# A fifth landing slot for weight pieces, and the on-chip space that it takes from constants, work tiles and step sizes

## The chip, the cores and the metric

The kernel runs on one core of a Trainium2 chip (trn2). A core has five engines that run side by side and wait for each other by semaphores: TensorE (PE; its weight loads are listed as PEld), VectorE (DVE), ScalarE (ACT), GpSimd (POOL) and SyncE (SP), which here mostly issues transfers. The metric is the device time of one execution in microseconds, the median of several runs.

## The reference, cut to what matters

Two layers over 256 rows of 1024 columns. A layer has a mixer, in which a retention branch and a state-space branch (SSD) run on the same normed input, and a gated feed-forward part.

```
for l in range(DEPTH):                                   # DEPTH = 2, x is (256, 1024), float32
    u = rmsnorm(h, norm_mix_w[l]) @ w_in[l]              # q, k, v, g_ret, z, xbc, dt, gate_ret, gate_ssd
    yr = retention(rotary(q), rotary(k) * DK**-0.5, v)   # 2 chunks of 128 rows, 4 heads
    o_ret = (silu(g_ret) * head_rmsnorm(yr)) @ ret_out[l]
    xs, bm, cm = split(silu(causal_dwconv(xbc)))
    dtp = softplus(dt + dt_bias);  a = -exp(a_log)       # "step sizes", 32 heads
    ys = ssd_scan(xs * dtp, dtp * a, bm, cm) + d_skip * xs
    o_ssd = (group_rmsnorm(ys * silu(z)) * ssd_norm_w[l]) @ ssd_out[l]
    h = h + (sigmoid(gate_ret) * o_ret + sigmoid(gate_ssd) * o_ssd) @ w_o[l]
    gate, up = split(rmsnorm(h, norm_ffn_w[l]) @ w_gate_up[l])
    h = h + (silu(gate) * up) @ w_down[l]
out = rmsnorm(h, final_norm_w)
```

## The kernel before, in words

All weights pass through the chip once. A weight piece is 128 partitions by up to 1024 columns (512 KB). Its way is: SyncE's queue issues its transfer into a landing tile (raw, line 488 in feeder); ScalarE copies it, rounded, into wh (line 508, split_h); VectorE subtracts, wl = raw - wh (line 533, split_l); TensorE multiplies three times with high and low halves (mm3, lines 550 to 552; the fm jobs in lines 1036 and 1039), which gives nearly float32 accuracy at the fast rate. A landing tile is free again when wl is written. Before, there are 4 landing tiles (RB) and 7 pairs of wh and wl (HB).

The work is a list of jobs, one per block of output columns: v, gr (the gates' and dt's columns), bc and xs (the convolved columns), q, k, g, z, then ret, ssd and wo (the three output products), and the FFN's. Each has matmul steps on TensorE and a "post" that drains its sums on ScalarE and VectorE. Three job kinds matter here:

- The ssd job (out_wino) and then the wo job (out_job). Post ssd_post multiplies and adds into D on VectorE (D<-acc,D and D<-D), TensorE transposes the block (tr<-cst,D, line 646 in transposed), ScalarE copies the high half (A<-tr) and VectorE subtracts for the low half (A<-tr,A). The wo job reads both halves.
- The z jobs. z_post takes a work tile (sil), writes silu into it, multiplies by the SSD result, normalises, and lets TensorE transpose it (tr<-cst,sil). At the same time the SSD chunks run: ips (line 1769) reads xdt, yps (line 1782) reads seg and xdt.
- A norm (class Norm). square takes a work tile for the sum of squares, half takes one for the normed block (sil<-O,rstd,wb), which is transposed into xT; "plain" is a further copy of the transposed block. Only when both ScalarE copies are made is the work tile free. This happens for four blocks (2 row halves t, 2 column halves n) at each norm, and in the opening, where x arrives in four blocks while the first v pair already runs on a transposed copy of x.

The order of the instructions on each engine is not written by hand. Class Flow plays the kernel at build time with a cost for every operation: a generator asks for an operation, an event, or a semaphore (a free tile), and whenever an engine is free the ready operation with the lowest priority number is emitted. What comes out is one fixed list per engine, and on the chip each engine goes through its list in order. So a change of the number of tiles changes the lists all along the kernel. The semaphores that the change touches are rawS (landing tiles), silS (work tiles "sil", 128x512) and the small tiles of steps().

steps() computes the step sizes: softplus of dt, la = -dt * exp(a_log), and its running sums by a product with the mask le (row index at most column index) and gt (its complement). ssd_scores multiplies three blocks of scores by le, ones, le.

Of the kernel before, what the change touches and what calls it, by code (L numbers as in the profile page):

```python
# [9 lines left out]
F32 = mybir.dt.float32  # L10
F32R = mybir.dt.float32r
AF = mybir.ActivationFunctionType
ALU = mybir.AluOpType
# [3 lines left out]
P = 128  # L17
D = 1024
SEQ = 256
NT = 2  # L20
# [4 lines left out]
NH = SG * HPG  # L25
M2 = NT * NH
# [14 lines left out]
    return [at, at + 2] if c < NPAIR else [at]  # L41


K_ID, K_GT, K_LE, K_COS, K_SIN, K_DEC = 0, 128, 256, 640, 896, 1152
K_N = K_DEC + RH * SEQ


# [145 lines left out]
def trunk_kernel(  # L193
# [3 lines left out]
    ssd_out, w_o, norm_ffn_w, w_gate_up, w_gf, w_rw, w_sw, w_dw, w_down, final_norm_w, consts, out,  # L197
):
    nc = tc.nc
    HB, RB, TAIL, WARM = 7, 4, 5, 2  # L200
    LATE = 2500.0
    SLOW, MT_SLACK = 1500.0, 800.0
    ADDS = 600.0
# [7 lines left out]
    tp = ctx.enter_context(tc.tile_pool(name="tp", bufs=2))  # L211
    sp = ctx.enter_context(tc.tile_pool(name="sp", bufs=2))
# [7 lines left out]
    def act(n, pr, out, in_, func, psum=False, **kw):  # L220
        ptr = sum(hasattr(kw.get(a), "shape") for a in ("scale", "bias"))
        cost = 0.833 * n + (50 if psum else 92) + 93 * ptr + (95 if "accum_out" in kw else 0)
        return Op("act", cost, lambda: nc.scalar.activation(out=out, in_=in_, func=func, **kw),  # L223
                  pr, TABLES.get(func))
# [4 lines left out]
    def tt(n, pr, out, in0, in1, op):  # L229
        return dve(n, pr, lambda: nc.vector.tensor_tensor(out=out, in0=in0, in1=in1, op=op))  # L230
# [21 lines left out]
    def pooled(pool_, shape, dt, tag, bufs):  # L252
        sem = Sem(bufs)
        return sem, lambda name=tag: pool_.tile(list(shape), dt, tag=tag, name=name, bufs=bufs)
# [3 lines left out]
    rawS, new_raw = pooled(wp, (P, D), F32, "raw", RB)  # L258
    hlS = Sem(HB)
    ccS, new_cc = pooled(tp, (P, D), F32, "cc", 2)  # L260
    silS, new_sil = pooled(tp, (P, 512), F32, "sil", 3)
    sxS, new_sx = pooled(tp, (P, 512), F32, "sx", 4)
    sxG = Sem(1)
    segS, new_seg = pooled(tp, (P, HPG, P), F32, "seg", 2)
# [10 lines left out]
    h = [None] * NT  # L275
    cst = cp.tile([P, K_COS], F32, tag="cst", name="cst")
    ident = cst[:, K_ID : K_ID + P]
    gt = cst[:, K_GT : K_GT + P]
    le = cst[:, K_LE : K_LE + P]
    ones = cst[:, K_LE + P : K_LE + 2 * P]  # L280
    mhalf = cp.tile([P, 2], F32, tag="mhalf", name="mhalf")
    junk = cp.tile([P, 2], F32, tag="junk", name="junk")

# [1026 lines left out]
    early_par = Event()  # L1310
    first_tables = []

    def layer(l, mix, nxt, opening=None):
# [38 lines left out]
        run["v01"] = lambda: first_pair(opening, [v_post(0), v_post(1)])  # L1352


        dps = sp.tile([P, M2], F32, tag="dps", name="dps", bufs=1)
        dt_ev = [Event() for _ in range(NT)]
        sgr, sgr_ev = [None] * NT, [[Event() for _ in range(3)] for _ in range(NT)]

# [24 lines left out]
        def small(tag):  # L1383
            return sp.tile([P, M2], F32, tag=tag, name=tag, bufs=1)
# [4 lines left out]
        def steps():  # L1389
            pr = at_job[0] + 2  # L1390
            _, prm = yield par
            ea = sp.tile([P, NH], F32, tag="ea", name="ea", bufs=1)
            yield dt_ev[0]
            yield dt_ev[1]
            ax, sr, pol, dtt = small("ax"), small("sr"), small("pol"), small("dtt")
            n = M2
            yield stt(n, pr, ax, dps, -1.0, dps, ALU.mult, ALU.max)
            yield act(n, pr, ax, ax, AF.Exp, scale=-1.0)
            yield act(NH, pr, ea, prm[:, 1, :], AF.Exp)

            yield ts(n, pr, sr, ax, 2.0, None, ALU.add)
            yield dve(6 * n, pr, lambda: nc.vector.reciprocal(out=sr, in_=sr))
            yield tt(n, pr, sr, ax, sr, ALU.mult)
            yield tt(n, pr, ax, sr, sr, ALU.mult)
            cf = [2.0 / (2 * i + 1) for i in range(9)]
            yield ts(n, pr, pol, ax, cf[8], cf[7], ALU.mult, ALU.add)
            for i in range(6, -1, -1):
                yield tt(n, pr, pol, pol, ax, ALU.mult)
                yield ts(n, pr, pol, pol, cf[i], None, ALU.add)
            yield tt(n, pr, pol, pol, sr, ALU.mult)  # L1410
            yield stt(n, pr, dtt, dps, 0.0, pol, ALU.max, ALU.add)
            la = small("pol")
            yield stt(n, pr, v3(la), v3(dtt), -1.0, ea.unsqueeze(1).broadcast_to([P, NT, NH]), ALU.mult, ALU.mult)
            yield 4000.0

            yield accS

            def sums():
                ps = new_acc()
                nc.tensor.matmul(ps[:, :M2], lhsT=le, rhs=la, start=True, stop=True)  # L1420
                nc.tensor.matmul(ps[:, M2 : M2 + NH], lhsT=gt, rhs=la[:, :NH], start=True, stop=True)
                return ps

            ps = yield pe(300, pr, sums)
            acs, dec = small("ax"), small("sr")
            yield dve(n, pr, lambda: nc.vector.tensor_copy(out=acs, in_=ps[:, :M2]))
            yield act(n, pr, dec, ps[:, NH : M2 + NH], AF.Exp, psum=True)
            fl.release(accS)
            yield accS

            def sums_t():
                ps = new_acc()
                for t in range(NT):
                    nc.tensor.matmul(ps[:NH, t * P : (t + 1) * P], lhsT=la[:, t * NH : (t + 1) * NH], rhs=le,
                                     start=True, stop=True)
                return ps

            ps = yield pe(490, pr, sums_t)
            yield silS
            acsT = new_sil("acsT")[:NH, : NT * P].rearrange("p (t i) -> p t i", t=NT)  # L1440
            yield act(SEQ, pr, acsT, ps[:NH, :SEQ].rearrange("p (t i) -> p t i", t=NT), AF.Copy, psum=True)
            fl.release(accS)

            def out_dma():
                dr = drp.tile([NT, NH, P], F32, tag="acs", name="acs")
                nc.sync.dma_start(out=dr.rearrange("t h i -> h t i"), in_=acsT)
                return dr

            dr = yield Op("sp", 100, out_dma, pr)
            yield 2500.0  # L1450
            fl.release(silS)
            fl.set(steps_ev, (dtt, acs, dec, dr))
# [237 lines left out]
        def ssd_scores(g):  # L1690
            pr = at_job[0]
            for w in range(2):
                yield bc_ev[w][g // 2]
            bT, cT = bc[0].value, bc[1].value
            yield LATE
            yield cbmS
            yield accS

            def scores():
                ps = new_acc("cps")  # L1700
                nc.tensor.matmul(ps[:, :SEQ], lhsT=bT[:, g, :P], rhs=cT[:, g, :], start=True, stop=True)
                nc.tensor.matmul(ps[:, SEQ : SEQ + P], lhsT=bT[:, g, P:], rhs=cT[:, g, P:], start=True, stop=True)
                return ps

            ps = yield pe(660, pr, scores)
            cb = sp.tile([P, 3, P], F32, tag="cbm", name="cbm", bufs=SG)
            yield tt(3 * P, pr, cb, ps[:, : 3 * P].rearrange("p (b i) -> p b i", b=3),
                     cst[:, K_LE : K_LE + 3 * P].rearrange("p (b i) -> p b i", b=3), ALU.mult)
            fl.release(accS)
            cb_left[0] -= 1  # L1710
            if not cb_left[0]:
                fl.release(bigS["D"])
                fl.release(bigS["D"])
            fl.set(cb_ev[g], cb)
# [451 lines left out]
    def whole():  # L2166
# [48 lines left out]
        def constants(lo, hi):  # L2215
            yield load(cst[:, lo:hi], consts[:, lo:hi])
            fl.transfer(4 * P * (hi - lo), 4 * (hi - lo))

        def norm_w():
            fl.spawn(norms[0].start(-1, "sp"))  # L2220
            yield 1.0

        def tables(i):
            fl.spawn(first_tables[i]())
            yield 1.0

        others = [x_half(t, n) for t in range(NT) for n in range(2)] + [
            constants(K_ID, K_GT), norm_w(), params(0, early_par), constants(K_GT, K_COS), tables(0), tables(1)]
        fl.spawn(opening.load(0))
        fl.spawn(feeder([*zip((2, 6, 7), (opening.load(i) for i in range(1, 4))), *zip(BESIDE, others)]))  # L2230
        for l in range(DEPTH):
# [7 lines left out]
def _constants(np):  # L2239
    f = np.float32  # L2240
    c = np.zeros((P, K_N), f)
    a = np.arange(P)
    c[:, K_ID : K_ID + P] = np.eye(P, dtype=f)
    c[:, K_GT : K_GT + P] = a[:, None] > a[None, :]
    c[:, K_LE : K_LE + P] = a[:, None] <= a[None, :]
    c[:, K_LE + P : K_LE + 2 * P] = 1.0
    c[:, K_LE + 2 * P : K_LE + 3 * P] = c[:, K_LE : K_LE + P]
    half = DK // 2
    inv = f(10000.0) ** (-np.arange(half, dtype=f) / f(half))
    ang = inv[:, None] * np.arange(SEQ, dtype=f)[None, :]  # L2250
    c[:, K_COS : K_COS + SEQ] = np.cos(ang)
    c[:, K_SIN : K_SIN + SEQ] = np.sin(ang)
    i = np.arange(SEQ)
    diff = i[None, :] - a[:, None]
    for hd in range(RH):
        lg = math.log(1.0 - 2.0 ** (-5.0 - hd))
        c[:, K_DEC + hd * SEQ : K_DEC + (hd + 1) * SEQ] = np.where(
            diff >= 0, np.exp(lg * np.maximum(diff, 0)) * DK ** -0.5, 0.0)
    return c
# [63 lines left out]
```

## Time and profile before

| | |
|---|---|
| median of 3 runs (lowest, highest) | 1258.3 us (1257.64, 1258.99) |
| the profiled execution | 1257.84 us |
| its span | 1255.6 us |
| granted TensorE clock, mean | 0.998 |
| busy: PE, DVE, ACT | 1239.3, 1104.5, 873.0 us |
| moved by DMA | 266.27 MB, mean 212 GB/s |

The profile comes from one execution. Its page gives busy times, groups of instructions by source line, and the chain that ended last; other views list who waited for whom, instructions in order of time, and sums over stretches of time. A line of the timeline has the start and the duration in us, the engine, the source line, the operation, the tiles written and read, and how many instructions were merged; in brackets the engine's idle time before it and what ended that. SPq rows are issues of transfers. The end of a matmul is modelled: the next one starts before the drawn end.

### The profile page before, as it was taken

To read this page: it belongs to the slowest core of one execution; us is meant where nothing else is said; L and a number is where in the kernel's file an instruction comes from. 1 tells how busy PE (TensorE), PEld (TensorE's weight loads), DVE (VectorE), ACT (ScalarE), POOL (GpSimd) and SP (SyncE) were. 2 spreads that over 40 slices of the span, in tenths; PEclk is the share of its full clock that TensorE was granted. 3 is DMA by queue.
4 is the path that set the end of the run, shared out by engine and by line. 5 is a ranking of instruction groups with operands and counts; after the bars stand their busy time and mean duration, and the time that the engine had idled before them with its cause. 6 is when DMAs were issued, how large, how long until landed. Compare 5 with 4: busy or idle time off the path is not lost.

```text
span 1255.6 us, 17609 instructions
## 1 busy us (share of the span) xinstructions
PE 1239.3 (99%) x6293; PEld 1051.0 (84%) x6293; DVE 1104.5 (88%) x1513; ACT 873.0 (70%) x1304; POOL 75.3 (6%) x92
## 2 busy tenths in 40 slices
PE   9999999999999999999999999999999999999998
PEld 7889888888878788888888898888888787888886
DVE  6988888989999979999788888879889998899996
ACT  6966878785856566776586676967957674776753
POOL 0000000001022001001000000000010120010010
PEclk9999999999999999999999999999999999999999
DMA  9748464466767647877776574555685676578872
GB/s 322 247 123 286 160 215 164 154 228 162 260 227 218 231 161 231 296 212 218 254 254 223 131 253 170 180 169 165 220 211 195 249 220 216 197 224 254 283 203 97
DMA packets 76343, 266.27 MB, mean 212 GB/s; under 512 B 8768, under 2 KB 9536, under 8 KB 76256
## 3 DMA queue, kind: packets, MB, share of 16 engines
q1 hardware_dynamic: 68272, 237.12, 54.9%
q0 software_dynamic: 7552, 27.38, 11.5%
q8 instruction: 49, 0.80, 0.2%
q10 hardware_dynamic: 432, 0.66, 0.1%
q14 instruction: 38, 0.31, 0.1%
HBM read 262.96 MB, written 2.16 MB: 211 GB/s over the span
## 4 chain that ended last, share of the span: by engine, by line
PE 70%; DVE 14%; issue 6%; DMA 5%; ACT 4%; POOL 1%; POOLq 0%; ACTq 0%; DVEq 0%; SPq 0%
PE acc L1036 15%; PE acc L550 14%; PE acc L552 14%; PE acc L551 14%; PE acc L1039 8%; DVE wl L533 6%; ACT wh L508 2%; PE yps L1782 2%; PE tr L646 2%; DVE D L230 1%; DMA raw<-in_w_fm_dram 1%; ACT seg L1746 1%; DMA raw<-in_w_rw_dram 1%; DVE cc L233 1%; DMA raws<-in_w_sw_dram 1%
## 5 line engine op out<-in xcount | busy, mean ns | idle before, releaser
L533 DVE TENSOR_TENSOR wl<-raw,wh 128x1024 fp32r<-128x1024 f32 (+2 forms) x387 | 458.4, 1196 | 56.1 <-ACT wh L508 54.5
L508 ACT ACTIVATE wh<-raw 128x1024 fp32r<-128x1024 f32 (+2 forms) x387 | 396.4, 1038 | 139.5 <-PE acc L552 40.9
L1036 PE MATMUL acc<-xT,wh 128*128 128x512 f32 x960 | 249.4, 394 | 0.0
L550 PE MATMUL acc<-wh,xT 128*128 128x512 f32 (+1 forms) x568 | 221.1, 389 | 0.0
L551 PE MATMUL acc<-wl,xT 128*128 128x512 f32 (+1 forms) x568 | 216.0, 380 | 0.4 <-DVE wl L533 0.4
L552 PE MATMUL acc<-wh,xT 128*128 128x512 f32 (+1 forms) x568 | 216.1, 381 | 0.0
L1036 PEld LDWEIGHTS acc<-xT,wh 128*128 128x128 f32 x960 | 171.0, 189 | 28.8
L1039 PEld LDWEIGHTS acc<-xT,wl 128*128 128x128 f32 x960 | 131.0, 190 | 9.4 <-issue 0.5
L1039 PE MATMUL acc<-xT,wl 128*128 128x256 f32 x960 | 137.0, 284 | 0.0
L551 PEld LDWEIGHTS acc<-wl,xT 128*128 128x128 f32 x568 | 106.8, 188 | 20.7 <-issue 1.2
L550 PEld LDWEIGHTS acc<-wh,xT 128*128 128x128 f32 x568 | 106.7, 188 | 20.0 <-issue 1.2
L552 PEld LDWEIGHTS acc<-wh,xT 128*128 128x128 f32 x568 | 106.7, 188 | 19.7
L508 ACT ACTIVATE wh<-raws 128x1024 fp32r<-128x1024 f32 x80 | 83.7, 1056 | 32.9 <-DVE raws L230 13.8
L533 DVE TENSOR_TENSOR wl<-raws,wh 128x1024 fp32r<-128x1024 f32 x80 | 96.6, 1220 | 9.0 <-ACT wh L508 8.4
L552 PE MATMUL acc<-wh,A 128*128 128x512 f32 x224 | 87.6, 391 | 3.2 <-DVE A L230 3.2
L550 PE MATMUL acc<-wh,A 128*128 128x512 f32 x224 | 88.6, 396 | 0.0
L551 PE MATMUL acc<-wl,A 128*128 128x512 f32 x224 | 87.2, 389 | 0.0
L233 DVE SCALAR_TENSOR_TENSOR cc<-cc,cv 128x255 f32<-128x255 f32 (+2 forms) x144 | 67.5, 478 | 7.5 <-ACT cc L223 6.8
L552 PEld LDWEIGHTS acc<-wh,A 128*128 128x128 f32 x224 | 42.0, 188 | 12.9 <-DVE A L230 4.0
L550 PEld LDWEIGHTS acc<-wh,A 128*128 128x128 f32 x224 | 42.1, 188 | 8.5 <-ACT sil L223 0.4
L223 ACT ACTIVATE sil<-acc 128x512 f32<-128x512 f32 (+1 forms) x60 | 31.0, 526 | 26.0 <-PE acc L552 14.1
L551 PEld LDWEIGHTS acc<-wl,A 128*128 128x128 f32 x224 | 42.1, 188 | 8.3
(200 smaller groups left out, 1999.7 us busy)
## 6 DMA issues: line engine op xcount, KB each, us to landing
raw<-in_w_tm_dram SPq DMA_DIRECT2D x100, 512.0 KB, 4.2
raw<-in_w_fm_dram SPq DMA_DIRECT2D x80, 512.0 KB, 4.2
raw<-in_w_gf_dram SPq DMA_DIRECT2D x40, 512.0 KB, 4.5
raw<-in_w_gate_up_dram SPq DMA_DIRECT2D x32, 512.0 KB, 5.4
raw<-in_w_down_dram SPq DMA_DIRECT2D x28, 512.0 KB, 4.4
raw<-in_w_gr_dram SPq DMA_DIRECT2D x24, 352.0 KB, 3.8
seg<-acs SPq DMA_DIRECT2D x16, 512.0 KB, 5.3
raw<-in_ret_out_dram SPq DMA_DIRECT2D x16, 512.0 KB, 5.0
```

What stands on the lines that cost most here:

```text
L223: return Op("act", cost, lambda: nc.scalar.activation(out=out, in_=in_, func=func, **kw), pr, TABLES.get(func))
L230: return dve(n, pr, lambda: nc.vector.tensor_tensor(out=out, in0=in0, in1=in1, op=op))
L233: return Op("dve", 1.04 * n + 130, lambda: nc.vector.scalar_tensor_tensor(out=out, in0=in0, scalar=scalar, in1=in1, op0=op0, op1=op1), pr)
L508: nc.scalar.activation(out=wh[:, :m], in_=raw[:, :m], func=AF.Copy)
L533: nc.vector.tensor_tensor(out=wl[:, :m], in0=raw[:, :m], in1=wh[:, :m].bitcast(F32), op=ALU.subtract)
L550: nc.tensor.matmul(ps, lhsT=lh, rhs=rh, start=first, stop=False, **kw)
L551: nc.tensor.matmul(ps, lhsT=lh, rhs=rl, start=False, stop=False, **kw)
L552: nc.tensor.matmul(ps, lhsT=ll, rhs=rh, start=False, stop=last, **kw)
L646: nc.tensor.transpose(out=ps[:, j * P : (j + 1) * P], in_=src[:, j * P : (j + 1) * P], identity=ident)
L1036: nc.tensor.matmul(box[0], lhsT=wh[:, k, fsl], rhs=x[:, k, :, :], start=(half, k) == (0, 0), stop=(half, k) == (1, 3))
L1039: nc.tensor.matmul(box[0][:, :SEQ], lhsT=wl[:, k, fsl], rhs=xh[:, k, :], start=False, stop=False)
L1782: nc.tensor.matmul(ps[:, i * HD : (i + 1) * HD], lhsT=sg[:, i, :], rhs=xdt[:, i * HD : (i + 1) * HD], start=True, stop=True)
```

## The change

It makes a fifth landing tile for weight pieces (4 KB in each partition) and frees space for it:

- The constants held on the chip shrink from 640 columns to 256: the identity and le stay. gt is made by VectorE as 1 - le, in a work tile called side, which is taken before the sums and then also holds the transposed sums (acsT). The blocks "ones" and the second le fall away: ssd_scores lets ScalarE copy the middle block and VectorE multiply the outer two by le.
- Two work tiles "sil" instead of three.
- steps() works in place: dps and dtt are one tile, and exp(a_log) is written over a_log.

```diff
-K_ID, K_GT, K_LE, K_COS, K_SIN, K_DEC = 0, 128, 256, 640, 896, 1152
+K_ID, K_LE, K_COS, K_SIN, K_DEC = 0, 128, 256, 512, 768
...
-    HB, RB, TAIL, WARM = 7, 4, 5, 2
+    HB, RB, TAIL, WARM = 7, 5, 5, 2
...
-    silS, new_sil = pooled(tp, (P, 512), F32, "sil", 3)
+    silS, new_sil = pooled(tp, (P, 512), F32, "sil", 2)
...
-        dps = sp.tile([P, M2], F32, tag="dps", name="dps", bufs=1)
+        dps = sp.tile([P, M2], F32, tag="dtt", name="dtt", bufs=1)
...
-            ea = sp.tile([P, NH], F32, tag="ea", name="ea", bufs=1)
+            ea = prm[:, 1, :]
...
-            ax, sr, pol, dtt = small("ax"), small("sr"), small("pol"), small("dtt")
+            ax, sr, pol, dtt = small("ax"), small("sr"), small("pol"), dps
...
+            yield silS
+            side = new_sil("side")
+            gt = side[:, SEQ : SEQ + P]
+            yield ts(P, pr, gt, le, -1.0, 1.0, ALU.mult, ALU.add)
...
-            yield silS
-            acsT = new_sil("acsT")[:NH, : NT * P].rearrange("p (t i) -> p t i", t=NT)
+            acsT = side[:NH, : NT * P].rearrange("p (t i) -> p t i", t=NT)
...
-            yield tt(3 * P, pr, cb, ps[:, : 3 * P].rearrange("p (b i) -> p b i", b=3),
-                     cst[:, K_LE : K_LE + 3 * P].rearrange("p (b i) -> p b i", b=3), ALU.mult)
+            yield act(P, pr, cb[:, 1, :], ps[:, P : 2 * P], AF.Copy, psum=True)
+            yield tt(2 * P, pr, cb[:, 0::2, :], ps[:, : 3 * P].rearrange("p (b i) -> p b i", b=3)[:, 0::2, :],
+                     le.unsqueeze(1).broadcast_to([P, 2, P]), ALU.mult)
...
-            constants(K_ID, K_GT), norm_w(), params(0, early_par), constants(K_GT, K_COS), tables(0), tables(1)]
+            constants(K_ID, K_LE), norm_w(), params(0, early_par), constants(K_LE, K_COS), tables(0), tables(1)]
```

The diff doesn't show how the lists of the engines change. Two places do, of those where TensorE waits. The lines of the file are two lower after the change (506 for 508, 531 for 533, 644 for 646).

ScalarE in the opening, layer 0, from the splits of the gr pieces on. wh<-raw 128x704 is the split of a gr piece, wh<-raw 128x1024 that of a conv piece and of those behind it; sil,ss<-O is a square, A<-acc,rstd a drain of the first v pair, xT<-tr and plain<-tr the two copies of transposed blocks. Before:

```order
L508 ACTIVATE wh<-raw 128x704
L223 ACTIVATE sil,ss<-O 128x512
L508 ACTIVATE wh<-raw 128x704
L223 ACTIVATE A<-acc,rstd 128x512 x2
L223 ACTIVATE xT<-tr 128x4x128 x2
L223 ACTIVATE sil,ss<-O 128x512
L223 ACTIVATE plain<-tr 128x512 x2
L508 ACTIVATE wh<-raw 128x1024
```

And after the change, at the same place:

```order
L506 ACTIVATE wh<-raw 128x704 x2
L223 ACTIVATE A<-acc,rstd 128x512 x2
L506 ACTIVATE wh<-raw 128x1024
L223 ACTIVATE xT<-tr 128x4x128 x2
L506 ACTIVATE wh<-raw 128x1024 x2
L223 ACTIVATE plain<-tr 128x512 x2
L223 ACTIVATE sil,ss<-O 128x512 x2
```

The two squares, of which one stood ahead of A and one ahead of plain, now stand together behind plain, and three splits of 1024 columns have moved ahead of xT and plain.

VectorE at the end of layer 0's mixer, where ssd goes over into wo. D<-D and D<-acc,D are ssd_post's sum and product, wl<-raw,wh are splits of w_o pieces and later ones, A<-tr,A the low half of a transposed block. Before:

```order
L230 TENSOR_TENSOR D<-D 128x512
L230 TENSOR_TENSOR D<-acc,D 128x512
L533 TENSOR_TENSOR wl<-raw,wh 128x1024
L230 TENSOR_TENSOR D<-D 128x512
L230 TENSOR_TENSOR D<-acc,D 128x512
L533 TENSOR_TENSOR wl<-raw,wh 128x1024
L230 TENSOR_TENSOR D<-D 128x512
L230 TENSOR_TENSOR A<-tr,A 128x4x128
L230 TENSOR_TENSOR D<-acc,D 128x512
L230 TENSOR_TENSOR A<-tr,A 128x4x128
```

And after:

```order
L230 TENSOR_TENSOR D<-D 128x512
L230 TENSOR_TENSOR D<-acc,D 128x512
L531 TENSOR_TENSOR wl<-raw,wh 128x1024
L230 TENSOR_TENSOR D<-D 128x512
L230 TENSOR_TENSOR D<-acc,D 128x512
L230 TENSOR_TENSOR A<-tr,A 128x4x128
L230 TENSOR_TENSOR D<-D 128x512
L230 TENSOR_TENSOR D<-acc,D 128x512
L531 TENSOR_TENSOR wl<-raw,wh 128x1024
L230 TENSOR_TENSOR A<-tr,A 128x4x128
```

Before, two splits stand between the second D<-D that feeds a transpose and the first A<-tr,A; after the change it is one, and the second split has moved behind that A. On TensorE the first transpose there has 9 matmuls behind it up to the second, where it had 6. Layer 1 has the same new order.

More of the change, by code (lines that the diff above doesn't have):

```diff
@@ L277, in trunk_kernel @@
     ident = cst[:, K_ID : K_ID + P]
-    gt = cst[:, K_GT : K_GT + P]
     le = cst[:, K_LE : K_LE + P]
-    ones = cst[:, K_LE + P : K_LE + 2 * P]
     mhalf = cp.tile([P, 2], F32, tag="mhalf", name="mhalf")
@@ L1398, in steps @@
             yield act(n, pr, ax, ax, AF.Exp, scale=-1.0)
-            yield act(NH, pr, ea, prm[:, 1, :], AF.Exp)
+            yield act(NH, pr, ea, ea, AF.Exp)
             yield ts(n, pr, sr, ax, 2.0, None, ALU.add)
@@ L2243, in _constants @@
     c[:, K_ID : K_ID + P] = np.eye(P, dtype=f)
-    c[:, K_GT : K_GT + P] = a[:, None] > a[None, :]
     c[:, K_LE : K_LE + P] = a[:, None] <= a[None, :]
-    c[:, K_LE + P : K_LE + 2 * P] = 1.0
-    c[:, K_LE + 2 * P : K_LE + 3 * P] = c[:, K_LE : K_LE + P]
     half = DK // 2
```

## The prediction

> **What bounds the kernel now.** I read the page first, then the list of what TensorE waited for, then the same list for ScalarE, and at the places that these name the timeline. The page's span and busy row:
>
> ```profile
> span 1255.6 us, 17609 instructions
> ...
> PE 1239.3 (99%) x6293; PEld 1051.0 (84%) x6293; DVE 1104.5 (88%) x1513; ACT 873.0 (70%) x1304; POOL 75.3 (6%) x92
> ```
>
> TensorE is idle for 1255.6 - 1239.3 = 16.3 us, ends of the span included. The change removes no large matmul and adds none, so it can gain only from these waits, and can lose by making new ones. The waits on TensorE that matter here (total, times, longest):
>
> ```profile
> PE acc L552 <- DVE A L230: 3.2, 2, 1.8
> ...
> PE ips L1769 <- DVE xdt L230: 1.3, 2, 1.0
> PE tr L646 <- ACT wh L508: 1.3, 1, 1.3
> PE tr L646 <- DVE sil L233: 0.9, 3, 0.3
> PE tr L646 <- DVE D L230: 0.7, 2, 0.4
> PE yps L1782 <- DVE Y L230: 0.5, 1, 0.5
> PE acc L551 <- DVE wl L533: 0.4, 1, 0.4
> ```
>
> Only the last of these is a wait for a weight piece: 0.4 us. The fifth landing slot works on another engine, which the list for ScalarE shows:
>
> ```profile
> ACT wh L508 <- PE acc L552: 51.9, 51, 3.0
> ...
> ACT wh L508 <- DMA raw<-in_w_tm_dram: 18.5, 15, 4.1
> ...
> ACT wh L508 <- DMA raw<-in_w_o_dram: 6.4, 6, 2.1
> ```
>
> ScalarE mostly waits for TensorE to free a split piece (51.9 us), and at some places for a landing. There the slot starts a transfer earlier; TensorE profits only where such a late piece sits in a queue in front of something that it needs.
>
> **The change part by part.**
>
> *Mixer's end (ssd job to wo job), both layers.* Four of the waits lie here: two for A (3.2 us) and two for D (0.7 us). The first, in layer 0:
>
> ```profile
> 425.28 0.63 PE L646 MATMUL tr<-cst,D 128*128 128x128 f32 x4 [0.28 <-DVE D L230]
> 425.66 1.21 DVE L533 TENSOR_TENSOR wl<-raw,wh 128x1024 fp32r<-128x1024 f32 x1
> ...
> 425.98 0.40 PE L551 MATMUL acc<-wl,A 128*128 128x512 f32 x1
> ...
> 426.79 0.68 DVE L230 TENSOR_TENSOR D<-D 128x512 f32<-128x512 f32 x1
> ...
> 427.39 0.68 DVE L230 TENSOR_TENSOR A<-tr,A 128x512 fp32r<-128x512 f32 x1
> ...
> 428.13 0.50 PE L552 MATMUL acc<-wh,A 128*128 128x512 f32 x1 [1.75 <-DVE A L230]
> ...
> 429.14 0.40 PE L551 MATMUL acc<-wl,A 128*128 128x512 f32 x1
> ...
> 429.37 0.40 PE L552 MATMUL acc<-wh,A 128*128 128x512 f32 x1
> ```
>
> The low half of the transposed block (A<-tr,A) sits on VectorE behind a split wl of 1.21 us and a D of 0.68 us. L551 and L552 start 2.15 us apart here and 0.23 us apart a little later, so the wait costs 1.92 us where the list says 1.75: a matmul's end is modelled, and 0.17 us is to be added to each wait. The four cost 3.9 + 4 x 0.17 = 4.6 us. In the changed order one split fewer stands between the transpose and its A, and the first transpose is issued three matmuls earlier. I count it through from the first transpose, at T: with the durations above, wl ends at T + 0.5, D, D<-acc and then A at T + 2.4 us; TensorE does 9 matmuls (2.0 us) and the second transpose (0.5 us) and comes to the matmul that reads A's low half at T + 3.4. So the wait goes, with a margin of 1 us; layer 1 has the same new order. What is late next: the splits of w_o, for which ScalarE waited 6.4 us; one slot more starts each of these pieces earlier. I keep 0.4 us of the 4.6. **Term: -4.2 us** (bounds 0, if the splits stay late, and -4.6).
>
> *The z jobs, both layers.* Two waits for xdt (1.3 us) and one for Y (0.5 us) stand on VectorE behind splits. With the 0.17 each they cost 2.3 us. The seg products are as long as the splits:
>
> ```profile
> 338.74 2.35 DVE L230 TENSOR_TENSOR seg<-seg,cbm 128x1024 f32<-128x1024 f32 x2
> ```
>
> In the new order the matmul ips comes two products (1.36 us) later against its neighbours, while VectorE has one split (1.21 us) more, one seg (2.35 / 2 = 1.18 us) less and one Y of 0.68 us more ahead of xdt: about 0.7 us better; and in layer 0 yps now stands ahead of the two groups of transposes for whose Y it waited. I take **-1.7 us** (bounds 0 and -2.3).
>
> *The opening.* Here the two work tiles bite. Before, a third tile lets the square of x's rows 128 to 255 run on ScalarE before the copies "plain"; with two, both tiles are held by the normed blocks until "plain" has read their transposes, so both squares stand behind it, and the split of the first conv piece (in_w_fm) now stands ahead of xT. Before:
>
> ```profile
> 27.71 1.03 PE L646 MATMUL tr<-cst,sil 128*128 128x128 f32 x8
> ...
> 28.50 0.40 PE L550 MATMUL acc<-wh,C 128*128 128x352 f32 x1
> ...
> 28.91 0.32 PE L552 MATMUL acc<-wh,C 128*128 128x352 f32 x1
> 29.07 0.32 PE L550 MATMUL acc<-wh,C 128*128 128x352 f32 x1
> ...
> 29.28 1.09 ACT L223 ACTIVATE xT<-tr 128x512 fp32r<-128x512 f32 x2
> ...
> 30.24 0.65 ACT L223 ACTIVATE sil<-O 128x512 f32<-128x512 f32 x1
> ...
> 30.76 0.22 ACT L223 ACTIVATION_READ_ACCUMULATOR sil<-O 128x1 f32 x1
> 31.11 1.19 ACT L223 ACTIVATE plain<-tr 128x512 f32<-128x512 f32 x2
> ...
> 32.20 1.05 ACT L508 ACTIVATE wh<-raw 128x1024 fp32r<-128x1024 f32 x1
> 32.47 1.41 DVE L233 SCALAR_TENSOR_TENSOR sil<-O,rstd,wb 128x512 f32<-128x512 f32 x2 [0.67 <-POOL rstd L243]
> ...
> 33.36 0.63 PE L646 MATMUL tr<-cst,sil 128*128 128x128 f32 x4 [1.26 <-ACT wh L508]
> ...
> 38.60 1.09 PE L1036 MATMUL acc<-xT,wh 128*128 128x512 f32 x4
> ```
>
> When does that conv piece land? Rows of the views by stretches of time and of DMA issues (the last three numbers of the first three rows are TensorE's granted clock, the share of time that the DMA engines were busy, and GB/s; the next two rows end in the median time from issue to landing, in us):
>
> ```profile
> 24.00:28.00 4.00, 4.00 (x21) 3.29 (x20) 2.37 (x4) 1.96 (x4) 0.03 (x1) 1.00 0.88 274
> 28.00:32.00 4.00, 4.00 (x28) 3.81 (x26) 3.53 (x6) 3.86 (x9) 0.12 (x1) 1.00 1.03 417
> 32.00:36.00 4.00, 2.74 (x20) 2.65 (x20) 3.54 (x5) 4.00 (x7) 0.43 (x1) 1.00 0.28 113
> ...
> raw<-in_w_fm_dram SPq DMA_DIRECT2D x2, 512.0 KB, 7.5
> cst<-consts_dram SPq DMA_DIRECT2D x1, 256.0 KB, 6.4
> ...
> 24.01 0.88 SPq L488 DMA_DIRECT2D raw<-in_w_fm_dram  x2
> ```
>
> Issued at 24.0 and 24.5 with a median of 7.5 us, 1.26 us apart at 417 GB/s, they land at about 31.1 and 32.4. The constants ahead of them shrink by 192 KB, 0.7 us at 274 GB/s. An earlier issue finds engines that are 0.88 busy already in these 4 us, so it fills at most 0.5 us. I take a landing at 29.9 us; the bounds are 28.4, where the whole slow stretch goes, and 31.1. Then on ScalarE: split 1.05, xT 1.09, two splits 2.1, plain 1.19, two squares of 0.87 each with their reads: end near 37.1. From a square's end (30.98) to the first transpose (33.36) it is 2.4 us, so the transposes start at about 39.4 less what overlaps, some 39. TensorE is there after 45 matmuls of 0.16 us from 28.5, at 35.7: a wait of about 3 us in place of 1.26, and behind it a wait for xT, which stands behind two splits and the pair A. L1036 starts near 41.4 instead of 38.60. **Term: +2.8 us** (bounds +1.0 and +4.8).
>
> [...]
>
> *Small new waits.* The pairs of transposes at the norms of the two FFNs and of layer 1 now stand side by side and wait for the second half (0.9 us in three such waits today), and in the first xs jobs ips of group 0 moves 9 us forward, to where VectorE has hardly an op of slack. I take **+1.0 us** (bounds 0 and 2).
>
> *Edits at nothing.* The middle block of the scores is copied by ScalarE instead of multiplied by ones on VectorE, eight times 128 columns; the mask gt is made twice from le, 128 columns; step sizes and the exponent of a_log are written in place. VectorE and ScalarE wait often there (88% and 70% busy), and TensorE reads the results many microseconds later. If that cover were gone, they would cost a few tenths each. The work tile taken earlier for gt keeps one of two tiles for some microseconds while no job in its place needs one.
>
> **The sum.** The profiled execution took 1257.84 us for a span of 1255.6, so 2.2 us lie outside, unchanged; it is 0.5 us below the median of the three runs, 1258.3. -4.2 - 1.7 + 2.8 + 1.0 = -2.1 us, so 1255.7 for that execution, **1256.2** against the median. A measurement of this kernel can tell about 0.2%, 2.5 us, from no change: the forecast lies just inside.
>
> **The rivals.**
> 1. *The slot does all that the order assumes.* The conv piece lands by 28.4 us, the opening costs 1.0 us, and nothing small is new: -4.2 - 1.7 + 1.0 = -4.9, 1253.4 us. For it: the order puts the split ahead of xT, which only pays if the piece is there. Against: the row with 0.88 DMA share. Chance 0.20.
> 2. *Slower: two work tiles chain the pairs.* At nine places in the order, the opening among them, two separate groups of four transposes have become one of eight, since with two work tiles the two halves of a pair are taken and freed together. If TensorE waits at each for the second half, that is one product on VectorE, 1.41 / 2 = 0.71 us: 6.4 us in place of the 1.0, so -4.2 - 1.7 + 2.8 + 6.4 = +3.3, 1261.6 us. It decides from 5.6 us of such waits on, eight of the nine: only there is the sum over 2.5. For it: VectorE at 88%. Against: today's waits for sil sum to 0.9 us. Chance 0.13.
> 3. *The slot gives nothing.* The splits of w_o stay in front of A, since transfers of the seg blocks and of w_sw share the queue: the 4.2 is not gained, +2.1, 1260.4 us. For it: no wait of TensorE repeats along the kernel, and the one wait for a weight piece is 0.4 us. Chance 0.15.
>
> [...]
>
> **How the numbers follow.** The forecast has 0.52, with its own spread of about 1.6 us, so 0.20 of it lies beyond -2.5 us and 0.32 inside. Faster by over 0.2%: 0.20 + 0.20 = 0.40. Within: 0.32 + 0.12 of the third rival = 0.44. Slower: 0.13 + 0.03 = 0.16. The range reaches from 1252.6, which takes in most of the first rival, to 1260.6, which takes in the third; the second is left out, and with the tail of the first that is under 0.2.
>
> **What would show it.** In the list of TensorE's waits: the rows for A and D of 3.9 us gone or under 0.5 (else the third rival); those for xdt and Y under 0.7; the opening's first L1036 at 41 to 42 us (at 40 or less: the first rival); waits for sil near 2 us (4 or more: the second). The forecast is wrong if L1036 starts before 39.6 or after 43.5, or if some wait over 2 us shows up at a place that is not named here.

## The result and the profile after

The changed kernel takes 1253.95 us (median of 7 runs, 1253.03 to 1255.08), the kernel before 1258.01 us beside it (7 runs, 1256.37 to 1258.99). The ratio is 0.9969 with a 95% interval of 0.9957 to 0.998: the medians differ by 4.1 us, the ratio says 0.31% faster. The whole interval lies below 1, and its near end is at the 0.2% that the prediction took for the least that can be told from no change. The forecast was 1256.2, the range 1252.6 to 1260.6.

The page's span and busy row after the change, and all waits of TensorE that it lists (total, times, longest):

```profile
span 1252.2 us, 17656 instructions
...
PE 1238.6 (99%) x6293; PEld 1052.0 (84%) x6293; DVE 1104.9 (88%) x1515; ACT 872.7 (70%) x1310; POOL 72.7 (6%) x92
```

```profile
PE acc L548 <- ACT sx L223: 3.7, 5, 0.9
PE idle L2198 <- DVE mhalf L2175: 1.3, 1, 1.3
PE acc L1034 <- DVE xT L230: 1.0, 1, 1.0
PE tr L644 <- DVE D L230: 0.6, 2, 0.3
PE tr L644 <- DVE sil L233: 0.3, 1, 0.3
```

The span is 3.4 us shorter. A (3.2 us), xdt (1.3), Y (0.5), wl (0.4) and C (0.3) have left the list; in the opening the transposes' wait for wh (1.3) has gone and a wait for xT (1.0) has come. What is new is the wait for sx, the drain of an accumulator on ScalarE: 0.2 us before, 3.7 now. Now the places, layer 0's mixer end first (the first transpose of D, VectorE's rows behind it, the matmul that reads the low half):

```profile
424.05 0.63 PE L644 MATMUL tr<-cst,D 128*128 128x128 f32 x4 [0.32 <-DVE D L230]
424.42 1.22 DVE L531 TENSOR_TENSOR wl<-raw,wh 128x1024 fp32r<-128x1024 f32 x1
...
425.56 0.68 DVE L230 TENSOR_TENSOR D<-D 128x512 f32<-128x512 f32 x1
...
426.16 0.69 DVE L230 TENSOR_TENSOR D<-acc,D 128x512 f32<-128x512 f32 x1
...
426.76 0.68 DVE L230 TENSOR_TENSOR A<-tr,A 128x512 fp32r<-128x512 f32 x1
...
427.50 0.50 PE L550 MATMUL acc<-wh,A 128*128 128x512 f32 x1
```

One split stands between the transpose and A, as the order said, and L550 doesn't wait. It is closer than it looks: A ends at 427.44, L550 starts at 427.50.

The opening (ScalarE, then TensorE), and the stretches by time in which its pieces land (the last three numbers are TensorE's granted clock, the DMA engines' share, GB/s):

```profile
28.48 1.06 ACT L506 ACTIVATE wh<-raw 128x1024 fp32r<-128x1024 f32 x1 [0.35 <-DVE Y L233]
...
29.45 1.07 ACT L223 ACTIVATE xT<-tr 128x512 fp32r<-128x512 f32 x2
...
36.41 1.29 PE L644 MATMUL tr<-cst,sil 128*128 128x128 f32 x8 [0.25 <-DVE sil L233]
...
39.22 1.20 PE L1034 MATMUL acc<-xT,wh 128*128 128x512 f32 x4 [1.02 <-DVE xT L230]
```

```profile
20.00:24.00 4.00, 4.00 (x19) 3.34 (x18) 3.42 (x7) 3.52 (x6) 0.41 (x1) 1.00 1.02 364
24.00:28.00 4.00, 4.00 (x20) 3.25 (x19) 3.24 (x5) 1.93 (x3) 0.15 (x1) 1.00 1.04 371
```

The split of the first conv piece starts at 28.48 and waited for VectorE's Y, not for the piece: it had landed. Before, the stretch from 24 to 28 us moved 274 GB/s at a DMA share of 0.88; now it moves 371.

The new wait, in layer 0 (two rows of ScalarE ahead of the drain, the drain, the matmul that needs its accumulator):

```profile
316.08 1.06 ACT L506 ACTIVATE wh<-raw 128x1024 fp32r<-128x1024 f32 x1 [3.00 <-DMA raw<-in_w_rw_dram]
317.05 2.44 ACT L1748 ACTIVATE seg<-seg,ax 128x128 f32<-128x128 f32 x8
319.39 0.57 ACT L223 ACTIVATE sx<-acc 128x512 f32<-128x512 f32 x1
...
320.02 0.50 PE L548 MATMUL acc<-wh,O 128*128 128x512 f32 x1 [0.81 <-ACT sx L223]
```

ScalarE waits 3.0 us for a landing and then takes eight differences of a seg block before it drains the accumulator. Before, at the same place, it waited nearly as long for the piece, but the drain stood ahead of the differences:

```profile
314.12 1.06 ACT L508 ACTIVATE wh<-raw 128x1024 fp32r<-128x1024 f32 x1 [2.84 <-DMA raw<-in_w_rw_dram]
315.16 0.60 ACT L223 ACTIVATE sx<-acc 128x512 f32<-128x512 f32 x1
...
318.50 2.44 ACT L1746 ACTIVATE seg<-seg,ax 128x128 f32<-128x128 f32 x8
```

### The profile page after: what moved, and what is told of

Read it like the earlier page. It is cut to its first block, busy times and chain, and to the rows that moved or that the text cites. A ratio compares the mean times of both kernels' runs of the same rounds, so it can differ in the third digit from the quotient of the medians.

```text
span 1252.2 us, 17656 instructions
## 1 busy us (share of the span) xinstructions
PE 1238.6 (99%) x6293; PEld 1052.0 (84%) x6293; DVE 1104.9 (88%) x1515; ACT 872.7 (70%) x1310; POOL 72.7 (6%) x92
## 4 chain that ended last, share of the span: by engine, by line
PE 69%; issue 2%; DVE 1%; DMA 1%; ACT 1%; POOLq 0%; POOL 0%; DVEq 0%; ACTq 0%
PE acc L548 15%; PE acc L550 15%; PE acc L549 15%; PE acc L1034 12%; PE acc L1037 6%; PE tr L644 2%; DMA raws<-in_w_sw_dram 1%; PE yps L1784 1%; DVE wl L531 1%; ACT wh L506 1%; DVE D L230 0%; PE ips L1771 0%; DVE sx L230 0%; PE tr L1671 0%; PE acc L1500 0%
## 5 line engine op out<-in xcount | busy, mean ns | idle before, releaser
L1034 PE MATMUL acc<-xT,wh 128*128 128x512 f32 x960 | 251.0, 395 | 1.0 <-DVE xT L230 1.0
L550 PE MATMUL acc<-wh,xT 128*128 128x512 f32 (+1 forms) x568 | 216.1, 380 | 0.0
L1034 PEld LDWEIGHTS acc<-xT,wh 128*128 128x128 f32 x960 | 170.3, 189 | 29.6 <-DVE xT L230 1.3
L1037 PEld LDWEIGHTS acc<-xT,wl 128*128 128x128 f32 x960 | 131.8, 190 | 9.9
L1037 PE MATMUL acc<-xT,wl 128*128 128x256 f32 x960 | 136.2, 283 | 0.0
L550 PEld LDWEIGHTS acc<-wh,xT 128*128 128x128 f32 x568 | 106.7, 188 | 19.6
L506 ACT ACTIVATE wh<-raws 128x1024 fp32r<-128x1024 f32 x80 | 83.9, 1057 | 46.9 <-DVE raws L230 16.5
L550 PE MATMUL acc<-wh,A 128*128 128x512 f32 x224 | 87.6, 391 | 0.0
L550 PEld LDWEIGHTS acc<-wh,A 128*128 128x128 f32 x224 | 42.0, 188 | 9.4 <-DVE A L230 0.5
L223 ACT ACTIVATE sx<-acc 128x512 f32<-128x512 f32 (+1 forms) x62 | 32.5, 525 | 25.0 <-PE acc L1034 14.2
```

The source lines that it names most:

```text
L506: nc.scalar.activation(out=wh[:, :m], in_=raw[:, :m], func=AF.Copy)
L550: nc.tensor.matmul(ps, lhsT=ll, rhs=rh, start=False, stop=last, **kw)
L1034: nc.tensor.matmul(box[0], lhsT=wh[:, k, fsl], rhs=x[:, k, :, :], start=(half, k) == (0, 0), stop=(half, k) == (1, 3))
L1037: nc.tensor.matmul(box[0][:, :SEQ], lhsT=wl[:, k, fsl], rhs=xh[:, k, :], start=False, stop=False)
```

## The experiments

Two theories. The first is the prediction's: the fifth landing tile brings the gain, at the mixer's end and in the z jobs, and the two work tiles cost something in the opening. The rival: what matters is the fixed list that the plan draws; any edit draws a new one, and the tile itself does little. Eleven runs, each with a ratio against the kernel before beside it (medians of 1257.7 to 1258.0 us):

| run | median us | ratio, 95% interval | waits for A / D / xdt / sx, us | first matmul on xT, us |
|---|---|---|---|---|
| kernel before | 1258.0 | 1 | 3.2 / 0.7 / 1.3 / 0.2 | 38.60 |
| changed kernel | 1253.95 | 0.9969 (0.9957, 0.998) | 0 / 0.6 / 0 / 3.7 | 39.22 |
| e1 slot back | 1258.71 | 1.0006 (0.9998, 1.0015) | 0 / 1.8 / 1.5 / 0 | 41.07 |
| e2 slot, old order | 1252.75 | 0.9959 (0.9947, 0.9971) | 0 / 1.7 / 1.0 / 0 | 39.07 |
| e3 space only | 1261.59 | 1.0035 (1.0023, 1.0048) | 3.2 / 0.8 / 1.8 / 0.2 | 39.83 |
| e4 two tiles only | 1255.4 | 0.9978 (0.9969, 0.9986) | 0 / 1.8 / 1.9 / 0 | 39.94 |
| e5 space, old plan | 1258.24 | 1.0003 (0.9994, 1.0012) | 2.8 / 0.8 / 2.0 / 0.3 | 38.09 |
| e6 slot, xT first | 1252.73 | 0.9957 (0.9945, 0.997) | 0 / 1.2 / 2.0 / 0 | 38.81 |
| e7 seg after sx | 1253.11 | 0.996 (0.9946, 0.9973) | 2.3 / 0.9 / 0.6 / 0 | 40.67 |
| e8 ips later | 1250.62 | 0.9939 (0.9926, 0.9951) | 0 / 1.2 / 0 / 0 | 38.84 |
| e9 D later | 1249.83 | 0.9936 (0.9923, 0.995) | 0 / 0.6 / 0 / 0.2 | 38.16 |
| e10 two splits | 1253.67 | 0.9964 (0.9951, 0.9976) | 3.5 / 0.7 / 0 / 0 | 38.49 |
| e11 changed again | 1254.0 | 0.997 (0.9958, 0.9981) | 0 / 0.6 / 0 / 3.3 | 40.02 |

The waits are totals of TensorE's list in one profiled execution, and so is the start of the first matmul on xT (L1036 in the kernel before and e4, L1034 in the others); 0 is no row.

**e1: the slot taken back.**

```diff
-    HB, RB, TAIL, WARM = 7, 5, 5, 2
+    HB, RB, TAIL, WARM = 7, 4, 5, 2
```

> The changed kernel with four landing tiles again; constants, two work tiles and step sizes as changed. Theory (the slot brings the gain, the two work tiles cost little): the waits for A and D at the mixer's end and for xdt and Y in the z jobs come back, 4.6 + 2.3 = 6.9 us, the new waits for sx (4.5 us) go with the slot, the opening loses 0.7 us or more: 1258.5 to 1261 us, so 1.000 to 1.003 of the time before. Rival (any new list draws its waits anew, the slot has no part in it): the waits turn up at other places, and the time lies anywhere from 1253 to 1262, with no wait for A at the mixer's end as likely as one.

1258.71 us: within the theory's time, but not by its waits. The waits for xdt are back and those for sx gone, as it said; those for A are not back, although there are four tiles. The opening lost most: the first matmul on xT at 41.07 us, and on top of it this:

```profile
38.26 1.29 PE L644 MATMUL tr<-cst,sil 128*128 128x128 f32 x8 [1.67 <-DVE sil L233]
...
41.07 2.07 PE L1034 MATMUL acc<-xT,wh 128*128 128x512 f32 x4 [1.51 <-DVE xT L230]
```

```profile
42.00:44.00 2.00, 2.00 (x8) 1.72 (x7) 2.00 (x3) 2.00 (x3) 0.00 (x0) 0.50 0.18 25
```

The granted clock is 0.50, and four matmuls of 512 columns take 2.07 us where they take 1.20 in the changed kernel.

**e2: five tiles on the chip, four in the plan.** This takes the order out of the question: the lists are those of e1, word for word.

```diff
-    rawS, new_raw = pooled(wp, (P, D), F32, "raw", RB)
+    rawS, new_raw = Sem(RB - 1), pooled(wp, (P, D), F32, "raw", RB)[1]
```

> Five landing tiles on the chip, while the plan of the order still counts four: each engine has word for word the list of the run with four tiles, and only the transfers can start earlier. Theory that the earlier landings themselves bring the gain: TensorE's waits fall by 3 us or more against the run with four tiles. Rival that the gain comes through the order that the planner makes of five tiles: within 0.8 us of the run with four tiles, although ScalarE's waits for landings fall from some 50 us to half of it.

1252.75 us, 6.0 us less than e1 (some 4 to 8 by the intervals). That is what the tile does by earlier landings alone, and the rival's "little" falls. The spans of the two profiled executions differ by 4.1 us (e2's is the slowest of its five, 1254.07 us), 2.0 of it up to the first matmul on xT. The split of the first conv piece, which waits for the landing in both, shows where they come from; here and in the stretches by time e1 stands first, then e2:

```profile
30.33 1.06 ACT L506 ACTIVATE wh<-raw 128x1024 fp32r<-128x1024 f32 x1 [1.29 <-DMA raw<-in_w_fm_dram]
```

```profile
28.33 1.06 ACT L506 ACTIVATE wh<-raw 128x1024 fp32r<-128x1024 f32 x1 [0.54 <-DMA raw<-in_w_fm_dram]
```

```profile
24.00:28.00 4.00, 4.00 (x20) 3.26 (x19) 2.28 (x4) 1.71 (x3) 0.00 (x0) 1.00 0.89 285
```

```profile
24.00:28.00 4.00, 4.00 (x22) 3.33 (x21) 2.96 (x5) 1.95 (x3) 0.00 (x0) 1.00 1.06 395
```

A part of the 6.0 us comes through the clock. Row by row of their common list, e2's lead grows from 2.0 us at the first matmul on xT to 3.1 us at the second group of L1037 (47.55 us in e1, 44.44 in e2), while the granted clock is at 0.50 for 6.8 us in e1 and for 3.4 us in e2. The mean granted clock is 0.996 or 0.997 in nine of e1's eleven executions and 0.999 in three of e2's five, so the other executions of e2 may have lost less than the profiled one; how large the part is in the medians stays open. An estimate of its most is 3.4 us, half of the 6.8.

And the changed kernel, whose plan knows of the fifth tile, is no better than e2, whose plan doesn't: the list drawn for five tiles gains the z jobs and pays for them with the waits for sx.

**e3: the space edits alone** (four landing tiles, three work tiles).

```diff
-    HB, RB, TAIL, WARM = 7, 5, 5, 2
+    HB, RB, TAIL, WARM = 7, 4, 5, 2
...
-    silS, new_sil = pooled(tp, (P, 512), F32, "sil", 2)
+    silS, new_sil = pooled(tp, (P, 512), F32, "sil", 3)
```

> Constants in 256 columns, gt made on the chip, the middle block copied by ScalarE, step sizes in place; four landing tiles and three work tiles as before. The prediction put these edits at nothing: 1257.5 to 1258.8 us, within 0.05% of the time before, with the waits for A, D, xdt and Y of the profile before in their places. Rival (192 KB less of constants moves the opening, or the lists move with the edits): 1 us or more off, either way.

1261.59 us, 3.8 us more than before: the prediction's "edits at nothing" failed, and the rival's "1 us or more off" holds. The waits for A, D and xdt are in their places; ScalarE's opening differs:

```profile
30.34 1.06 ACT L506 ACTIVATE wh<-raw 128x1024 fp32r<-128x1024 f32 x1 [0.54 <-DVE Y L233]
...
31.31 1.07 ACT L223 ACTIVATE xT<-tr 128x512 fp32r<-128x512 f32 x2
```

The split of the conv piece stands ahead of xT, with three work tiles. The prediction read this move in the changed list and put it to the two tiles. Here it is the constants, as e5 below shows: the plan counts 128 columns where it counted 512, thinks that the piece lands earlier, and puts its split first; xT goes from 29.28 us to 31.31.

**e4: the two work tiles alone**, on the kernel before.

```diff
-    silS, new_sil = pooled(tp, (P, 512), F32, "sil", 3)
+    silS, new_sil = pooled(tp, (P, 512), F32, "sil", 2)
```

> The kernel before with two work tiles instead of three and nothing else. By the prediction's opening term with the conv piece landing at about 31 us (its upper bound) the first L1036 starts near 43 us and the run loses 3 to 5 us: 1261 to 1263. If the two tiles cost as little as in the changed kernel (0.7 us in the opening), 1258 to 1259.5. Rival of the chained pairs: waits for sil of 4 us or more, 1262 or more.

1255.4 us: all three expectations missed, it is 2.4 us faster than before. The waits for A are gone with four landing tiles:

```profile
PE tr L646 <- DVE sil L233: 2.1, 2, 1.8
PE ips L1769 <- DVE xdt L230: 1.9, 2, 1.0
PE tr L646 <- DVE D L230: 1.8, 2, 1.2
```

The opening pays 1.3 us for the two tiles (39.94 against 38.60), which is less than the waits for A. So the prediction's largest term does not come from the slot. It comes with the list that the plan draws when there are two work tiles: one split between the transpose and A, as in the changed kernel.

**e5: e3 with the plan's old cost of the constants.**

```diff
-            fl.transfer(4 * P * (hi - lo), 4 * (hi - lo))
+            cols = 512 if lo else hi
+            fl.transfer(4 * P * cols, 4 * cols)
```

> As the run with the space edits alone (four landing tiles, three work tiles; it lost 3.8 us), but the plan goes on charging the second transfer of the constants with 512 columns, while 128 are moved. In the opening every engine then has the list of the kernel before again: xT stands ahead of the split of the first conv piece. If that moved split is what the space edits cost, the time is back at 1257.3 to 1258.8 us and the opening's loss with it; the rival, that the copy of the middle block, gt or the steps in place cost it, leaves 1260 us or more.

1258.24 us. The code of the edits costs nothing, as predicted; their plan cost 3.8 us in e3.

**e6: e2 with that plan.**

```diff
-    rawS, new_raw = pooled(wp, (P, D), F32, "raw", RB)
+    rawS, new_raw = Sem(RB - 1), pooled(wp, (P, D), F32, "raw", RB)[1]
...
-            fl.transfer(4 * P * (hi - lo), 4 * (hi - lo))
+            cols = 512 if lo else hi
+            fl.transfer(4 * P * cols, 4 * cols)
```

> Five landing tiles on the chip, the plan counts four, and it charges the constants with their old size: xT stands ahead of the split of the first conv piece again, everything else as in the run with five tiles and the old order (1252.75). If that split ahead of xT costs in the opening even where its piece lands at 28 us, the opening loses 1 to 2 us less: 1250.8 to 1252 us. If the piece is there in time the split costs nothing: 1252.3 to 1253.3.

1252.73 us, the same as e2. Where the piece is there, the split ahead of xT costs nothing that shows in the median. That is weaker than it looks, since the rest did not stay as it was: the lists differ further on as well, the waits for xdt are 1.0 us longer and those for D 0.5 us shorter. In the opening alone the first matmul on xT comes 0.3 us earlier. (In e2's profiled execution the granted clock is at 0.50 for 3.4 us, in e6's it is 1.00; more on that at the end.)

e6 also gives a second price of the tile. Up to that matmul it has e4's lists on TensorE, ScalarE and VectorE, and there the granted clock is 1.00 in both profiles: five tiles bring it to 38.81 us where four have 39.94, and the medians are 1252.73 and 1255.4. That is 2.7 us (some 1 to 4 by the intervals), with the caution that the lists differ further on and that the two ran on different chips.

**e7: seg behind the drain**, on the changed kernel.

```diff
+            if g == SG - 1 and t == 0:
+                yield 2000.0
             yield Op("act", HPG * (0.833 * P + 185), differences, lp)
```

> The changed kernel, but the plan holds the eight differences of one seg block (2.44 us on ScalarE) back by 2 us, so that in both layers the drain sx<-acc stands ahead of them; lists outside this stretch are the same. If these 2.44 us in front of the drain make TensorE's new waits for sx (320.0, 326.7, 938.8 and 945.5 us, 3.8 us in all), 1250 to 1251.5 us. If the late w_rw piece in front of both makes them whatever the order, 1253.3 to 1254.5 us.

1253.11 us (1251.34 to 1255.03): between the two. The list of waits, from the slowest of the five, settles more than the time:

```profile
PE acc L550 <- DVE A L230: 2.3, 2, 1.2
PE tr L644 <- DVE sil L233: 1.6, 2, 1.2
...
PE tr L644 <- DVE D L230: 0.9, 2, 0.5
PE ips L1773 <- DVE xdt L230: 0.6, 2, 0.3
```

No row for sx: the seg block ahead of the drain made those waits, although the w_rw piece is as late as ever. But the lists did not stay the same elsewhere, as the expectation has it: they are drawn anew up to the mixer's end, with two splits ahead of A, and A is back.

**e8, e9, e10: single moves in the list of e6.** Each moves TensorE's rows by a few matmuls (the "products" of these expectations are single matmuls, those of the prediction groups of three); e8 and e9 leave the other engines' lists as they are.

```diff
                 x0 = yield x0_ev
+                if g == SG - 1:
+                    yield 1500.0
```

> On the run with five tiles and xT first (1252.73): the plan holds the matmul ips of the last group back, so that in both layers it stands six products (1.36 us) later in TensorE's list; the lists of VectorE, ScalarE and SyncE don't change by a row. If the two waits for xdt (2.0 us in the list, 2.3 us with the modelled ends) come from ips standing too early, they go and the time is 1250.3 to 1251 us. If VectorE is simply late there, and the matmuls behind ips wait for something of it in its stead, 1252.3 us or more.

1250.62 us, 2.1 us less than e6, and no row for xdt is left in the list. ips stood too early.

```diff
-            yield from transposed(sgr[t][:, nsl], 4, mT, n, t, j - 1, slack=MT_SLACK)
+            yield from transposed(sgr[t][:, nsl], 4, mT, n, t, j - 1, slack=MT_SLACK + 500 * (t == n == 0))
```

> On top of that, the first transpose of D stands three products (0.68 us) later in TensorE's list, in both layers; all else is the same list. The two waits for D (1.2 us in the list, 1.5 us with the modelled ends) fall to 0.2: 1249 to 1250 us. The margin ahead of the matmul that reads A was put at 1 us by the prediction's count, so no wait for A comes back; if that margin was less than 0.7 us, one does, and nothing is won.

1249.83 us (1249.5 to 1251.56), inside the expected times, but its 0.8 us against e8 are within the spread of the runs. The waits for D fell to 0.6, not 0.2: the second transpose waits in the first one's place.

```diff
-            yield from transposed(sgr[t][:, nsl], 4, mT, n, t, j - 1, slack=MT_SLACK + 500 * (t == n == 0))
+            yield from transposed(sgr[t][:, nsl], 4, mT, n, t, j - 1, slack=MT_SLACK + 1100 * (t == n == 0))
```

> The same with the first transpose of D three products later still. The plan then draws VectorE's list at the mixer's end as it was in the kernel before: two splits between the D that feeds the transpose and the first A<-tr,A instead of one. Theory (the second split makes the wait for A): the two waits for A are back, 2.5 to 3.5 us, and the time is 2 to 3 us above the run without this step. Rival (the wait for A went with the landing slot, which stays here): no wait for A, within 0.7 us of that run.

1253.67 us, 3.8 us above e9, more than the 2 to 3 us expected. The waits for A are back, with five landing tiles:

```profile
422.34 0.60 PE L644 MATMUL tr<-cst,D 128*128 128x128 f32 x4
...
423.24 0.69 DVE L230 TENSOR_TENSOR D<-D 128x512 f32<-128x512 f32 x1
...
424.44 1.22 DVE L531 TENSOR_TENSOR wl<-raw,wh 128x1024 fp32r<-128x1024 f32 x1
...
425.57 0.69 DVE L230 TENSOR_TENSOR D<-D 128x512 f32<-128x512 f32 x1
...
426.18 0.68 DVE L230 TENSOR_TENSOR A<-tr,A 128x512 fp32r<-128x512 f32 x1
...
426.92 0.50 PE L550 MATMUL acc<-wh,A 128*128 128x512 f32 x1 [1.75 <-DVE A L230]
```

From 422.11 to 423.33 VectorE is in the first split, the second starts at 424.44, and A is ready 1.75 us late. Not all of this is the second split: without its 1.22 us A would end at 425.64, and L550 could have started at 425.17, so that by this estimate some 0.5 us come from the later transpose. Four landing tiles without these waits (e1, e4) and five with them (e7, e10): the list decides here, and in each of the lists with the wait (before, e3, e5, e7, e10) two splits stand between the D that feeds the first transpose and its A, in both layers; in all others it is one.

**e11: the changed kernel again**, beside e8 to e10.

> The changed kernel itself once more, on the chip and against the runs of these three: 1253 to 1255 us, to compare them with it directly; the waits for sx (3.7 us) in the same places. The opening tells whether the fast transfers of 20 to 28 us (364 and 371 GB/s) are its rule.

1254.0 us, sx 3.3 us; against it e9 is 4.2 us faster on the same chip. The two stretches have 393 and 341 GB/s, so the fast transfers are there again, but the first matmul on xT comes at 40.02 us, 0.8 us later than in the first profile.

Five landing tiles with three work tiles were not tried.

## Why the prediction was right, and where it was not

By terms, from the two profiled executions, with the 0.17 us that the prediction adds to each wait:

| term | predicted us | measured us | working |
|---|---|---|---|
| mixer's end (A, D) | -4.2 | -3.6 | 3.9 to 0.6, and 2 x 0.17 |
| z jobs (xdt, Y) | -1.7 | -2.3 | 1.8 to 0, and 3 x 0.17 |
| opening | +2.8 | +0.6 | 38.60 to 39.22 (in e11 40.02, so +1.4) |
| small new waits: sil | +1.0 | -1.4 | 0.9 to 0 (the 0.3 left lies in the opening), and 3 x 0.17 |
| not in the sum: sx | 0 | +4.2 | 0.2 to 3.7, and 4 x 0.17 |
| not in the sum: wl, C | 0 | -1.0 | 0.7 to 0, and 2 x 0.17 |
| sum | -2.1 | -3.5 | the spans differ by 3.4 |

*Mixer's end and z jobs: right in place, near in size, and right to count the order; the order does not come from the slot.* Counting splits between a transpose and its reader, as the prediction did, fits the wait for A in every list. The count of the margin was off: wl starts 0.37 us after the transpose instead of ending at T + 0.5, so A ends at T + 3.4 and the margin is 0.06 us, not 1 us. And the gain was booked under the slot (third rival: "The slot gives nothing", so A stays). e4 and e10 show that slot and A are independent. Without a hand on ips the waits for xdt went only in the list drawn for five tiles, and e8 shows why: ips has to stand some six matmuls later, which are the two products that the prediction counted. That the slot is worth nothing, the same rival's claim, fails by e2 against e1: 6.0 us.

*The opening: the step that failed is "An earlier issue finds engines that are 0.88 busy already in these 4 us, so it fills at most 0.5 us."* The piece was issued at 22.17 us, where it was 24.01 before, and it had landed by 28.48 us, not at 29.9: that is the first rival's opening. By the prediction's own signs it was wrong here, as L1034 starts before 39.6 us (39.22; in e11 it is 40.02). A share of 0.88 at 274 GB/s was not a full queue: with the fifth tile the same stretch carries 371 at a share of 1.04. From e1 to e2 it goes from 285 to 395 GB/s (39% more) while the share goes from 0.89 to 1.06 (19% more), so here the share alone did not tell how much more could be moved. The cost itself was real: with four tiles the same lists of ScalarE and VectorE pay it (e1: 41.07). In the opening the slot does not so much gain as pay for what the edits that make room for it cost.

*Small new waits: the wrong place.* The prediction looked for them at the pairs of transposes, and the second rival was built on it: sil fell to 0.3 us, and that in the opening. They came at the drains sx, 3.7 us in all, which the order showed and the prediction didn't speak of: a seg block of 2.44 us had moved ahead of the drain. A wait of over 2 us at a place that is not named was one of its own signs of being wrong; as a row it is that, though no single one of the five is over 0.9 us.

*Edits at nothing: right for the instructions (e5), wrong for the plan (e3).* A transfer made smaller moves a split in the list.

So the sum came out 1.4 us too high: the opening 2.2 too dear, sil 2.4, wl and C 1.0, the z jobs 0.6, less 4.2 for sx that was not seen and 0.6 at the mixer's end. The medians differ by 4.1 us, the two profiled executions by 3.9 and their spans by 3.4: some 0.4 us of the gain lie outside the span, where the prediction had 2.2 us unchanged (1.8 after). The large errors cancel, and that is luck: the range held, but not because each term did. The measured time is nearer to the first rival's 1253.4 us than to the forecast's 1256.2; that rival had the landing right and an opening of 1.0 us, but "nothing small is new" was wrong by the waits for sx.

## What to carry to other kernels

Where a planner turns sizes into fixed lists, an edit has two effects, on the chip and on the lists, and they can be measured apart: give the chip the new buffer and the plan the old count. Here the buffer was worth 6.0 us in one list, a part of it through the clock, and some 2.7 us in another (e4, e6); the list drawn for it gave nothing more. Then read the lists at the places where the bounding engine waits, count what stands ahead of what it waits for, and move single rows: with five tiles under the plan for four, the constants' old cost in the plan and two steps moved in TensorE's list (e9), the time is 1249.8 us, 0.64% (0.5 to 0.77) under the kernel before.

## What the runs showed of the hardware

**The clock fell in two runs, behind the opening's transposes.** In e1 and e2, and in no other of the profiled executions, the granted clock went to 0.50 after the opening's transposes. e2, by stretches and in TensorE's rows:

```profile
40.00:42.00 2.00, 2.00 (x10) 1.81 (x9) 2.00 (x3) 2.00 (x3) 0.00 (x0) 0.50 0.15 16
```

```profile
36.26 1.29 PE L644 MATMUL tr<-cst,sil 128*128 128x128 f32 x8
39.07 1.85 PE L1034 MATMUL acc<-xT,wh 128*128 128x512 f32 x4 [1.51 <-DVE xT L230]
```

These two share a list in which no other matmul stands between the eight transposes and the first matmul on xT; in all others at least three stand there, and their granted clock is 1.00 from 26 to 50 us, with single waits of up to 1.83 us (e4). From the last matmul ahead of the transposes to that on xT it is 4.5 us in e1 and 2.8 us in e2. By stretches of 1 us the granted clock is 0.50 for 6.8 us in e1 (40.1 to 46.9 us) and for 3.4 us in e2 (39.4 to 42.8 us). No run changed this place alone, so what makes the clock fall was not shown.

The prediction's sum has no term for the clock, and for the changed kernel that holds: the granted clock is 1.00 in the opening in both its profiles.

**The slow stretch of the opening is not the rule of four tiles alone.** From 20 to 28 us the four-tile kernels moved 238 to 316 GB/s, five-tile ones 320 to 396, but the profiled execution of e7, with five tiles, has

```profile
24.00:28.00 4.00, 4.00 (x20) 3.30 (x19) 2.30 (x3) 0.62 (x2) 0.53 (x1) 1.00 0.90 292
```

and its first matmul on xT is at 40.67 us. Why it moves less there is open; the runs of e7 spread over 3.7 us.
